# Two gate projections of a convolution branch in blocks of seven products, and a z gate applied four heads later

## The chip, the core and the metric

The kernel is one decoder layer for 256 tokens, and runs on one core of a Trainium2 chip. The metric is the device time of the core in microseconds; 1037.4 us is the median of three runs of the kernel before (1037.0 to 1037.94).

## The reference

All arithmetic is float32. A normalised input `h` (256 x 2048) is projected by one wide matrix, and the pieces feed two branches, attention over 16 heads and a short causal convolution with three taps. Each branch has a gate, and two further gates merge the branches:

```python
proj = jnp.einsum('bsd,de->bse', h, w_in)
# q_a, c_kv, k_rope, z_mla, c_in, b_gate, c_gate, z_conv, g_mla, g_conv = split(proj)
attn = _causal_mla_attention(q_nope, q_rope, k_nope, k_rope, v)      # 16 heads of 128
attn = attn.reshape(b, s, MLA_WIDTH) * jax.nn.silu(z_mla)
y_mla = jnp.einsum('bse,ed->bsd', attn, w_o_mla)
u = c_gate * c_in
conv = sum(conv_w[k] * u_pad[:, k:k + s] for k in range(CONV_K))
y_conv = jnp.einsum('bse,ed->bsd', b_gate * conv * jax.nn.silu(z_conv), w_o_conv)
merged = jax.nn.sigmoid(g_mla) * y_mla + jax.nn.sigmoid(g_conv) * y_conv
out = jnp.einsum('bsd,de->bse', merged, w_out)
x = x + _rmsnorm(out, post_norm_g)
```

The pieces that matter here are the seven projections of 2048 columns each: `z_mla`, `c_gate`, `c_in`, `z_conv`, `b_gate`, `g_mla`, `g_conv`.

## The kernel before, in words

**Three matmuls for a product.** TensorE works on pairs (hi, lo) of a rounded part and a rest. `product` (L253) issues three matmuls of 128 x 512 for one product: hi by hi, hi by lo, lo by hi. Each megabyte of weights (a unit) is loaded by SP into one of three `raw` buffers; ScalarE (ACT) copies it to `whi` (L269) and VectorE (DVE) subtracts to get `wlo` (L270). `whi` and `wlo` have three buffers each, and `take(i)` asks for the split of unit i+1 before unit i is used (`ahead`, L228). So the split of a unit can begin when the unit three places ahead of it has been used up, and must be done when its own turn comes.

**Plain projections.** A projection of 512 columns for all tokens is four units (quarters); each quarter is 2 token tiles x 4 k x 3 = 24 matmuls (`quarter`, L688). It fills two PSUM banks, one per token tile, which its evacuation must free before the next such projection can write them: the tag `cv` has two banks.

**The heads' stage** (L822 to 908) runs 16 heads. Each head's scores, softmax, transposition (by DVE in 32 x 32 pieces, then out to DRAM and back by DMAs of the POOL queue: `turned`, L345) and `values` leave TensorE nothing to do for long stretches, so plain projections are put between: before each four heads one projection of `z` (`gates`), and in each head the four quarters of one projection of the convolution branch (`channels`), in the order c_gate, c_in, z_conv, b_gate. A projection is evacuated in `channels_done` (L727): c_gate by a scaled copy on ACT; c_in and b_gate by a multiplication on DVE (L737); z_conv by a sigmoid on ACT (L734) and then L737 on DVE, so that both engines read its banks. `z` goes in the same way (L706, L707) into the very place of the attention output, is turned, and `values` multiplies each head's result into it (L682). The taps (`taps`) bring shifted rows and tap weights by POOL's DMAs and combine them on DVE (L770).

**Blocks of seven products.** The merge gates `g` (L956, `gate_block`, four blocks of 1024 columns) use a scheme that takes, for a pair of k (a "pair" unit), seven products in place of eight; a "whole" unit takes eight. A pair unit needs more splitting: `split_pair` (L204) makes three more weight sums `tf` on DVE (L212) and splits these too (`thi`, `tlo`). `gate_kinds` says which of a block's eight units are pairs: two in the first block, three in each of the others. All four blocks lie behind the heads, and their results `sg` stay in SBUF.

**Then** come the output projections of both branches (`sq`, 768 matmuls), the merge, and the last projection (`out`). A scheduler sets the order of instructions of an engine where `keep_in_program_order` does not; each engine then works strictly in that order.

## Time and profile before

| | |
|---|---|
| median of 3 runs | 1037.4 us |
| the profiled execution | 1037.89 us |
| its span | 1036.1 us |
| TensorE (PE) busy | 1022.2 us, 4661 matmul records |
| VectorE busy | 738.4 us |
| ScalarE busy | 530.6 us |
| POOL busy | 180.9 us |
| heads' stage | about 98 to 599 us |
| merge gates' blocks | 599.9 to 767 us |
| output projections `sq` | 767.2 to 941.3 us |

The profile shows one execution; the span is what the instructions cover, and the 1.8 us between it and the execution's time lie around them. In a group of instructions "busy" counts overlapping instructions once, and the mean is that of one instruction's own duration. A wait is put down to the instruction that released it.

### The profile page before, as it was taken

The numbers are of one execution on the slowest core, as the hardware profiler recorded it, in microseconds if no ns is written. First come the engines' busy times: TensorE is split into PE (matmuls) and PEld (weight loads), VectorE is DVE, ScalarE is ACT, GpSimd is POOL, SyncE is SP. The second block draws the span as 40 slices with busy tenths as digits, with TensorE's granted clock in tenths as the row PEclk, the third lists the DMA queues.
The fourth block names the chain that finished last, engine by engine and source line by source line (L and its number), as shares of the span: only waits on it lengthen the run. The fifth ranks groups of instructions, "written<-read, shape, count | busy, mean of one in ns | idle before, by whom it ended". The sixth has DMA issues, their size and how long they took to land.

```text
span 1036.1 us, 12480 instructions
## 1 busy us (share of the span) xinstructions
PE 1022.2 (99%) x4661; PEld 851.2 (82%) x4661; DVE 738.4 (71%) x960; ACT 530.6 (51%) x681; POOL 180.9 (17%) x345
## 2 busy tenths in 40 slices
PE   9999999999999999999999999999999999999997
PEld 8887888888888888888888888888888888888885
DVE  7578768776777767686678798898885455656562
ACT  7756546545556455464554645464664333443451
POOL 7620320204211241212222220000000000322000
PEclk9999999999999999999999999999999999999999
DMA  8755766668576676757576665555555555776842
GB/s 326 310 183 199 249 194 232 202 220 286 200 251 218 203 247 222 244 210 257 188 287 226 240 233 204 206 201 203 203 203 203 185 185 206 240 251 239 318 163 81
DMA packets 41948, 231.00 MB, mean 223 GB/s; under 512 B 7520, under 2 KB 8224, under 8 KB 18976
## 3 DMA queue, kind: packets, MB, share of 16 engines
q1 hardware_dynamic: 29808, 197.54, 53.5%
q0 software_dynamic: 11648, 29.38, 9.1%
q10 hardware_dynamic: 432, 3.29, 0.8%
q8 instruction: 36, 0.59, 0.2%
q14 instruction: 24, 0.20, 0.1%
HBM read 214.48 MB, written 11.53 MB: 218 GB/s over the span
## 4 chain that ended last, share of the span: by engine, by line
PE 95%; DVE 3%; issue 1%; ACT 1%; DVEq 0%; POOL 0%; POOLq 0%
PE cv L90 32%; PE sq L90 17%; PE g L90 16%; PE z L90 8%; PE out L90 8%; PE qa L90 2%; PE qn L90 2%; PE ckv L90 2%; PE kn L90 2%; PE vv L90 2%; DVE wlo L270 1%; PE sc L90 1%; PE o L90 1%; PE qr L90 1%; ACT whi L269 0%
## 5 line engine op out<-in xcount | busy, mean ns | idle before, releaser
L270 DVE TENSOR_TENSOR wlo<-raw,whi 128x1024 fp32r<-128x1024 f32 (+2 forms) x279 | 398.5, 1452 | 213.3 <-ACT whi L269 212.3
L269 ACT ACTIVATE whi<-raw 128x1024 fp32r<-128x1024 f32 (+2 forms) x281 | 336.4, 1233 | 344.2 <-issue 104.9
L90 PE MATMUL cv<-whi,x_both 128*128 128x512 f32 x1024 | 323.4, 390 | 2.9 <-DVE cv_w L737 2.9
L90 PEld LDWEIGHTS cv<-whi,x_both 128*128 128x128 f32 x1024 | 192.3, 188 | 43.1 <-DVE cv_w L737 4.0
L90 PE MATMUL cv<-wlo,x_both 128*128 128x512 f32 x512 | 199.7, 390 | 0.0
L90 PE MATMUL g<-whi,x_both 128*128 128x512 f32 x380 | 122.4, 389 | 0.0
L90 PEld LDWEIGHTS cv<-wlo,x_both 128*128 128x128 f32 x512 | 96.2, 188 | 18.7
L90 PEld LDWEIGHTS g<-whi,x_both 128*128 128x128 f32 x380 | 71.4, 188 | 14.7
L90 PE MATMUL z<-whi,x_both 128*128 128x512 f32 x256 | 80.6, 390 | 0.0
L90 PE MATMUL sq<-whi,x_both 128*128 128x512 f32 x256 | 79.0, 389 | 0.0
L90 PE MATMUL sq<-whi,cv_both 128*128 128x512 f32 x256 | 79.0, 389 | 0.0
L90 PE MATMUL out<-whi,x_both 128*128 128x512 f32 x256 | 79.0, 389 | 0.0
L356 POOL DMA_DIRECT2D far<-via x64 | 35.3, 558 | 223.8 <-DVE via L349 222.9
L90 PE MATMUL g<-wlo,x_both 128*128 128x512 f32 x190 | 73.9, 389 | 0.0
L356 POOL DMA_DIRECT2D far<-sg x32 | 17.5, 552 | 301.7 <-DVE sg L1045 259.7
L90 PEld LDWEIGHTS sq<-whi,x_both 128*128 128x128 f32 x256 | 48.1, 188 | 10.0
L90 PEld LDWEIGHTS sq<-whi,cv_both 128*128 128x128 f32 x256 | 48.1, 188 | 10.0
L90 PEld LDWEIGHTS out<-whi,x_both 128*128 128x128 f32 x256 | 48.1, 188 | 9.9
L90 PEld LDWEIGHTS z<-whi,x_both 128*128 128x128 f32 x256 | 48.1, 188 | 9.9
L90 PE MATMUL z<-wlo,x_both 128*128 128x512 f32 x128 | 49.8, 389 | 0.0
L90 PE MATMUL sq<-wlo,x_both 128*128 128x512 f32 x128 | 49.8, 389 | 0.0
L90 PE MATMUL sq<-wlo,cv_both 128*128 128x512 f32 x128 | 49.8, 389 | 0.0
(241 smaller groups left out, 1356.4 us busy)
## 6 DMA issues: line engine op xcount, KB each, us to landing
raw<-wcv_dram SPq DMA_DIRECT2D x64, 1024.0 KB, 5.3
raw<-wsq_dram SPq DMA_DIRECT2D x48, 1024.0 KB, 4.8
raw<-wg_dram SPq DMA_DIRECT2D x32, 1024.0 KB, 4.7
raw<-wz_dram SPq DMA_DIRECT2D x16, 1024.0 KB, 4.8
raw<-wqk_dram SPq DMA_DIRECT2D x8, 1024.0 KB, 5.9
cw<-cwr_dram POOLq DMA_DIRECT2D x24, 256.0 KB, 6.4
raw<-wc_dram SPq DMA_DIRECT2D x4, 1024.0 KB, 10.0
raw<-wv_dram SPq DMA_DIRECT2D x4, 1024.0 KB, 5.2
```

Of the source, the lines that this page charges most:

```text
L90: return tc.keep_in_program_order(nc.tensor.matmul(*a, **kw))
L269: a = nc.scalar.activation(hi, src, AF.Copy)
L270: b = nc.vector.tensor_tensor(lo, src, hi.bitcast(F32), op=ALU.subtract)
L356: tc.keep_in_program_order(nc.gpsimd.dma_start(out=f[i], in_=m))
```

## The change

`z_conv` and `b_gate` are no longer computed between the heads. Of the five plain projections with four parts each, three stay (`z`, `c_gate`, `c_in`): twelve projections of 512 columns (`FILLS`), four quarters ahead of the heads, two to three in each head. `z_conv` and `b_gate` become four blocks of 1024 columns in front of the four of the merge gates (`BLOCKS`), all by the scheme with seven products; `PLACES` gives each block's pair units (1, 3, 3, 2, 2, 3, 3, 3). In a pair unit DVE's two splits now stand one behind the other.

`z` is now evacuated by one activation (Silu, into `z_now`), turned in two steps, and multiplied into the attention output by `gates_weigh` four heads after its own four; the last one inside the first block. `values` no longer multiplies. The taps' steps are placed anew and take both token tiles with one load of the tap weights. The gate of the convolution branch, `w` = silu(z_conv) x b_gate, is a tile of 256 x 2048; the product of the convolution with it and its transposition move to the `sq` stage (`channels_steps`). The merge gates leave SBUF: each of 16 tiles is written to DRAM by POOL's queue (`gate_far`) and read back two at a time in the `sq` stage (`gate_tiles`).

The core of the diff:

```diff
+    order = ["fill"] * 4 + first
...
+        if u == "fill":
+            f, i = divmod(len(u_fill), 4)
+            j, n = FILLS[f]
+            u_fill.append(add(wz[j, i] if n == 2 else wcv[2 * j + n, i]))
         else:
-            u_head[i][j] = add(wcv[i, j])
...
         nc.scalar.activation(hi[:, :512], t[:, :512], AF.Copy)
-        split_act(thi[:, :, :], tlo[:, :, :], tf[:, :, :])
-        nc.vector.tensor_tensor(lo[:, :], t[:, :], hi[:, :].bitcast(F32), op=ALU.subtract)
+        nc.scalar.activation(thi[:, :, :], tf[:, :, :], AF.Copy)
+        tt(lo[:, :], t[:, :], hi[:, :].bitcast(F32), op=ALU.subtract)
+        tt(tlo[:, :, :], tf[:, :, :], thi[:, :, :].bitcast(F32), op=ALU.subtract)
...
-        f = temp("f")
-        whole(f[:, :], o)
-        nc.vector.tensor_tensor(at, f[:, :].rearrange("p (t i x) -> p t i x", t=NT, i=4), at, op=ALU.mult)
+        t = temp("half")
+        nc.scalar.activation(t[:, :], o[:, S:], AF.Copy)
+        a, b = (v.rearrange("p (t i x) -> p t i x", t=NT, i=4) for v in (o[:, :S], t[:, :]))
+        nc.vector.tensor_tensor(at, a, b, op=ALU.add)
...
-            cv_ps["now"] = [bank(f"cv{h}_{t}", tag="cv", bufs=2) for t in range(NT)]
-        quarter(cv_ps["now"], take(u_head[h][i]), i)
-        if i == 3:
-            channels_done(*divmod(h, 4))
-
-    def channels_done(j, n):
-        for t in range(NT):
-            ps, r = cv_ps["now"][t], r_col[:, t : t + 1]
-            w, u = cv_w[:, t, :], cv_t[:, j, t, :]
+            cv_ps["now"] = [bank(f"cv{f}_{t}", tag="cv", bufs=2) for t in range(NT)]
+        quarter(cv_ps["now"], take(u_fill[f]), i, between)
...
             if n == 0:
                 nc.scalar.activation(u, ps[:, :], AF.Copy, scale=r)
-            elif n == 2:
-                nc.scalar.activation(w, ps[:, :], AF.Sigmoid, scale=r)
-            if n:
-                dst = u if n == 1 else w
-                nc.vector.scalar_tensor_tensor(dst, ps[:, :], r, dst, op0=ALU.mult, op1=ALU.mult)
-
...
-    def channels_join(j, t):
-        u, w = cv_t[:, j, t, :], cv_w[:, t, :]
-        nc.vector.tensor_tensor(u, u, w, op=ALU.mult)
-
-        via = temp("cw", (P, 512), bufs=2) if t else temp("mv2", (P, 512), bufs=1, tag="mv2x")
-        go, come = turned(u, via, 4)
-        go()
-        return lambda: come(u)
...
+            elif n == 1:
+                nc.vector.scalar_tensor_tensor(u, ps[:, :], r, u, op0=ALU.mult, op1=ALU.mult)
+            else:
+                nc.scalar.activation(z_now[:, t, :], ps[:, :], AF.Silu, scale=r)
+        if n == 1:
+            steps = taps(j)
+            tap_steps.extend([steps] * 3 if j == 3 else [steps, None, steps, None, steps])
+        elif n == 2:
+            z_steps.append(gates_turn())
...
+    def gates_turn():
+        steps = [turned(z_now[:, t, :], temp("via", (P, 512), bufs=2), 4) for t in range(NT)]
+        for go, _ in steps:
+            go()
+        yield
+        for t, (_, come) in enumerate(steps):
+            come(z_now[:, t, :])
+        yield
+
+    def gates_weigh(v):
+        for t in range(NT):
+            at = at_t[:, v, t, :]
+            tc.keep_in_program_order(nc.vector.tensor_tensor(at, at, z_now[:, t, :], op=ALU.mult))
...
+            fill()
         if h < H - 1:
             score(h)
         if h:
-            channels(h, 0)
...
+            fill()
...
+        step()
         for i in made[h]:
             make(*i)
+        if h > 1 == at:
+            make("v", v)
+            pt = turn(ps_by_head.pop(h - 1))
...
+        if h < H - 1:
+            arrive()
...
+        fill()
...
+        if h and not h > 1 == at:
+            pt = turn(ps_by_head.pop(h - (h < H - 1)))
+        if v and at == HV - 1:
+            gates_weigh(v - 1)
...
+        step()
+        if h and not h > 1 == at:
+            fill()
+        if h:
+            values(h - (h < H - 1), pt)
...
+        for job in jobs.get(len(kinds), ()):
+            job()
         for m, t, half, other in ((2, 0, 0, p1[:, :]), (3, 0, 1, u[:, 0]), (4, 1, 0, u[:, 2]), (0, 1, 1, u[:, 1])):
-            o = 1024 * b + 512 * half
-            g = sg[:, n, t, o : o + 512]
-            tt(g, ps[m][:, :], other, op=ALU.add)
-            nc.scalar.activation(g, g, AF.Sigmoid, scale=r_col[:, t : t + 1])
...
+            done(ps[m][:, :], other, t, half)
...
+    def open_spool():
+        bstack.close()
+        sp = main.enter_context(tc.tile_pool(name="sp", bufs=1, side="right"))
+        spool["pool"] = sp
+        spool["w"] = sp.tile([P, NT, D], F32, name="cv_w")
...
+    def zc_done(b):
+        def done(ps, other, t, half):
+            o = D // 2 * b + 512 * half
+            silu(spool["w"][:, t, o : o + 512], ps, other, t)
+
+        return done
+
+    def b_done(b):
+        def done(ps, other, t, half):
+            o = D // 2 * b + 512 * half
+            w = spool["w"][:, t, o : o + 512]
+            nc.vector.tensor_tensor(other, ps, other, op=ALU.add)
+            nc.vector.scalar_tensor_tensor(w, other, r_col[:, t : t + 1], w, op0=ALU.mult, op1=ALU.mult)
+
+        return done
...
+    def g_done(n, b):
+        def done(ps, other, t, half):
+            c = 2 * b + half
+            g = spool["pool"].tile([P, 512], F32, name=f"sg{n}{c}{t}", tag="sg", bufs=4)
+            nc.vector.tensor_tensor(g[:, :], ps, other, op=ALU.add)
+            nc.scalar.activation(g[:, :], g[:, :], AF.Sigmoid, scale=r_col[:, t : t + 1])
+            gate_far[n, c, t] = dram.tile([P, 512], F32, name=f"gate{n}{c}{t}", tag=f"gate{n}{c}{t}", bufs=1)
+            tc.keep_in_program_order(nc.gpsimd.dma_start(out=gate_far[n, c, t][:, :], in_=g[:, :]))
+
+        return done
...
+    jobs = {1: [gates_step], 2: [gates_step], 5: [lambda: gates_weigh(NV - 1)], 7: [open_spool]}
+    for n, (name, b) in enumerate(BLOCKS):
+        put = g_done(*divmod(b, 2)) if name == "g" else {"zc": zc_done, "b": b_done}[name](b)
+        if n == len(BLOCKS) - 1:
+            jobs = {6: [lambda: split_branch(0), lambda: split_branch(1)], 7: [lambda: split_branch(2)]}
+        block(n, put, jobs)
+        jobs = {}
...
+    def channels_steps(i):
+
+        if i < 8:
+            j, t = divmod(i, NT)
+            u = cv_t[:, j, t, :]
+            w = spool["w"][:, t, 512 * j : 512 * j + 512]
+            tc.keep_in_program_order(nc.vector.tensor_tensor(u, u, w, op=ALU.mult))
+            go, channels_come[i] = turned(u, spool["pool"].tile([P, 512], F32, name="via_c", tag="via", bufs=2)[:, :], 4)
+            go()
+        if 2 <= i < 10:
+            j, t = divmod(i - 2, NT)
+            channels_come.pop(i - 2)(cv_t[:, j, t, :])
+        if 5 <= i < 13:
+            split_channels(i - 5)
...
+            if n == 0:
+                channels_steps(4 * c + kk)
...
+    def gate_tiles(n, c):
+        gs = []
+        for t in range(NT):
+            g = spool["pool"].tile([P, 512], F32, name=f"gs{n}{c}{t}", tag="sg", bufs=4)
+            tc.keep_in_program_order(nc.gpsimd.dma_start(out=g[:, :], in_=gate_far[n, c, t][:, :]))
+            gs.append(g[:, :])
+        return gs
...
+FILLS = [(0, 0), (0, 1), (1, 0), (1, 1), (0, 2), (2, 0), (2, 1), (1, 2), (3, 0), (2, 2), (3, 1), (3, 2)]
+BLOCKS = [("zc", 0), ("zc", 1), ("b", 0), ("b", 1), ("g", 0), ("g", 1), ("g", 2), ("g", 3)]
+PLACES = [(4,), (0, 2, 4), (0, 2, 4), (0, 3), (0, 3)] + [(0, 2, 4)] * 3```

Where a projection's banks are freed. Before, on DVE, at the end of a z_conv projection, that of head 6 counted from 0 (L737 reads the two banks `cv_0` and `cv_1`; `mv` and `cw` are taps, `f` and `half` are evacuations of q, k and v parts, `pt` are the turned weights of a head):

```order
L270 TENSOR_TENSOR wlo_2781<-raw_2745,whi_2780 128x1024 x2
L770 TENSOR_TENSOR cv_f<-cv_f,cw 128x512
L270 TENSOR_TENSOR wlo_2853<-raw_2778,whi_2852 128x1024 x2
L770 TENSOR_TENSOR cv_f<-cv_f,mv_2583 128x512
L423 TENSOR_TENSOR f<-qr_2753,half 128x256
L270 TENSOR_TENSOR pt<-p,pt 128x384
L737 SCALAR_TENSOR_TENSOR cv_w<-cv_0_2627,r_both,cv_w 128x512
L737 SCALAR_TENSOR_TENSOR cv_w<-cv_1_2628,r_both,cv_w 128x512
```

Now the two-engine evacuation is gone from the heads; this is ACT at the end of a z projection, the nearest thing to it:

```order
L268 ACTIVATE pt<-p 128x384
L268 ACTIVATE whi_2190<-raw_2096 128x512
L716 ACT_TABLE_LOAD
L716 ACTIVATE z_now<-cv_0_1827,r_both 128x512
L716 ACTIVATE z_now<-cv_1_1828,r_both 128x512
L268 ACTIVATE whi_2228<-raw_2188 128x1024 x2
L680 ACTIVATE half<-o_2144 128x256
```

The two banks are read by two activations of one engine, with a table load in front.

Ahead of the scores of the first head, on DVE, up to the split of `qr`, which the scores need. Before:

```order
L270 TENSOR_TENSOR wlo_951<-raw_908,whi_950 128x1024
L270 TENSOR_TENSOR kn<-f,kn 128x256
L270 TENSOR_TENSOR vv_lo<-vv_0_916,vv_hi 128x512
L270 TENSOR_TENSOR kn<-f,kn 128x256
L423 TENSOR_TENSOR f<-qr_881,half 128x256
L270 TENSOR_TENSOR vv_lo<-vv_1_931,vv_hi 128x512
L486 TENSOR_TENSOR rp_a<-f,cos_t 128x256
L489 TENSOR_TENSOR rp_b<-f,sin_t 32x256 x4
L270 TENSOR_TENSOR wlo_1025<-raw_948,whi_1024 128x1024 x2
L490 TENSOR_TENSOR f<-rp_a,rp_b 128x256
L270 TENSOR_TENSOR wlo_1065<-raw_1022,whi_1064 128x512
L270 TENSOR_TENSOR qr<-f,qr 64x256 x2
```

And now, on the same engine and at the same place:

```order
L269 TENSOR_TENSOR wlo_949<-raw_906,whi_948 128x512
L422 TENSOR_TENSOR f<-kn_0_840,half 128x256
L422 TENSOR_TENSOR f<-kn_1_841,half 128x256
L269 TENSOR_TENSOR vv_lo<-vv_0_914,vv_hi 128x512
L269 TENSOR_TENSOR kn<-f,kn 128x256 x2
L422 TENSOR_TENSOR f<-qr_879,half 128x256
L485 TENSOR_TENSOR rp_a<-f,cos_t 128x256
L488 TENSOR_TENSOR rp_b<-f,sin_t 32x256 x4
L269 TENSOR_TENSOR vv_lo<-vv_1_929,vv_hi 128x512
L489 TENSOR_TENSOR f<-rp_a,rp_b 128x256
L269 TENSOR_TENSOR wlo_1015<-raw_946,whi_1014 128x1024 x2
L269 TENSOR_TENSOR qr<-f,qr 64x256 x2
```

Behind the split of the unit ahead of these rows (`wlo_911` before, `wlo_909` now) stood two quarters of 2 x 1024 (`wlo_951`, whose first half stands two rows above the excerpt, and `wlo_1025`) and one half-unit of 512; now one quarter (`wlo_1015`) and one half-unit of 512. One quarter's split no longer stands in front of `qr`.

In the blocks, on DVE, at the border of two blocks. Before (first to second block; L1000 frees the first block's banks, `tf` and `raw` are a pair unit's sums):

```order
L212 TENSOR_TENSOR tf_5700<-raw_5669 128x1024
L1000 TENSOR_TENSOR sg<-g_4_5381,u 128x512
L1000 TENSOR_TENSOR sg<-g_0_5384,u 128x512
L212 TENSOR_TENSOR raw_5669<-raw_5669,tf_5700 128x512
L212 TENSOR_TENSOR tf_5700<-raw_5669 128x512
L220 TENSOR_TENSOR wlo_5699<-raw_5669,whi_5698 128x2048
L270 TENSOR_TENSOR wlo_5738<-raw_5696,whi_5737 128x2048
L270 TENSOR_TENSOR tlo_5702<-tf_5700,thi_5701 128x1536
```

And now, from the first `b_gate` block to the second, where each of four evacuations has a second operation (L983):

```order
L210 TENSOR_TENSOR wlo_4981<-raw_4948,whi_4980 128x2048
L210 TENSOR_TENSOR tlo_4984<-tf_4982,thi_4983 128x1536
L982 TENSOR_TENSOR p_4911<-g_2_4749,p_4911 128x512
L269 TENSOR_TENSOR wlo_5036<-raw_4978,whi_5035 128x2048
L983 SCALAR_TENSOR_TENSOR cv_w<-p_4911,r_both,cv_w 128x512
L982 TENSOR_TENSOR u<-g_3_4750,u 128x512
L982 TENSOR_TENSOR u<-g_4_4748,u 128x512
L982 TENSOR_TENSOR u<-g_0_4751,u 128x512
L983 SCALAR_TENSOR_TENSOR cv_w<-u,r_both,cv_w 128x512 x3
L269 TENSOR_TENSOR wlo_5063<-raw_5033,whi_5062 128x2048
```

The `tlo` of a pair unit, which stood behind the next unit's `wlo`, now stands directly behind its own; three second operations stand behind the last bank's read and in front of the next split.

264 lines of the change are left out of this document (105 added, 159 removed).

## The prediction

> **What bounds the kernel now.** First the page's table of busy times and its row of the granted clock:
>
> ```profile
> PE 1022.2 (99%) x4661; PEld 851.2 (82%) x4661; DVE 738.4 (71%) x960; ACT 530.6 (51%) x681; POOL 180.9 (17%) x345
> PEclk9999999999999999999999999999999999999999
> ```
>
> TensorE is busy for 1022.2 of 1036.1 us, so what is left outside it is 13.9 us, and no other engine comes near. Whether that busy time is work is told by its waits:
>
> ```profile
> PE cv L90 <- DVE cv_w L737: 2.9, 4, 0.9
> PE sc L90 <- DVE qr L270: 1.7, 1, 1.7
> PE idle L90 <- POOL hpi L293: 1.1, 1, 1.1
> PE g L90 <- DVE tlo L270: 0.4, 1, 0.4
> ```
>
> These are all (total, times, longest): 6.1 us; the other 7.8 us are the end, behind the last matmul (941.30 + 87.05 = 1028.35 in the next view). Four waits of up to 0.9 us stand at the release of a projection's banks, one at the first head's scores, one in the blocks. The chain of work that ended last gives the price of one matmul, and the table of stages (span, PE, PEld, DVE, ACT, POOL busy, clock, DMA share, GB/s) what cover there is in each:
>
> ```profile
> 767.22 174.08 PE sq L90 x768
> 941.30 87.05 PE out L90 x384
> 233.00:369.00 136.00, 135.16 (x635) 113.09 (x635) 100.71 (x162) 72.25 (x110) 29.33 (x54) 1.00 0.68 229
> 599.90:766.70 166.80, 166.41 (x735) 137.48 (x734) 145.55 (x123) 91.82 (x78) 5.48 (x10) 1.00 0.59 208
> 767.20:941.30 174.10, 174.10 (x770) 144.21 (x769) 100.40 (x77) 70.98 (x51) 16.43 (x30) 1.00 0.60 212
> ```
>
> 174.08 / 768 = 0.2267 us from matmul to matmul. The second row is one round of four heads; the third the merge gates' blocks, where VectorE is already busy for 145.55 / 166.8 = 87% and TensorE waited 0.4 us.
>
> **TensorE's own work.** Before: 16 + 4 plain projections of 96 matmuls (1920), and four blocks of 192 less 3 for each of 11 pairs (735), 2655 together. Now 12 projections (1152) and eight blocks with 20 pairs (1536 - 60 = 1476), 2628. All are 128 x 512. 27 fewer at 0.2267 us: **-6.1 us**, on the path, since TensorE has next to no idle time to absorb it. The Trainium skill (TensorE: Matmul & The Clock Gate, "Back-to-back issue gap") gives a sustained spacing of about 131 ns for matmuls of 512 columns; the trace disagrees with its 227 ns, and it decides. By the page's figure the term would be an estimated -3.5 us.
>
> **Waits that go.** The release of a z_conv projection's banks, in the chain and on the two engines that free them:
>
> ```profile
> 301.88 3.40 PE cv L90 x15
> 305.28 0.95 PE sc L90 x8
> 306.26 0.75 DVE cv_w L737
> 307.06 0.96 PE cv L90 x3
> 303.12 1.28 ACT L734 ACT_TABLE_LOAD   x1
> 304.42 0.69 ACT L734 ACTIVATE cv_w<-cv,r_both 128x512 f32<-128x512 f32 x1
> 305.80 0.55 DVE L270 TENSOR_TENSOR pt<-p,pt 128x384 fp32r<-128x384 f32 x1
> ```
>
> The first bank is complete 12 matmuls (2.7 us) ahead of 305.28, at 302.6. A table load and the sigmoid end at 305.1, then VectorE is at other work until 306.26, and its multiplication lets TensorE in at 307.06. Two engines in a row are longer than the 2.7 + 0.95 us of cover. z_conv leaves the heads, so these four waits go: **-2.9 us** (bounds -2.9 and 0, if others come in their place; those I count below). z is now freed by ACT alone: 1.28 + 0.69 = 2.0 us, under 2.7.
>
> For the first scores, VectorE's queue:
>
> ```profile
> 83.24 2.36 DVE L270 TENSOR_TENSOR wlo<-raw,whi 128x1024 fp32r<-128x1024 f32 x2 [0.57 <-ACT whi L269]
> 93.50 2.36 DVE L270 TENSOR_TENSOR wlo<-raw,whi 128x1024 fp32r<-128x1024 f32 x2
> 96.83 0.87 DVE L270 TENSOR_TENSOR qr<-f,qr 64x256 fp32r<-64x256 f32 x2
> ```
>
> From 83.24 to `qr` it is busy without a break, and one quarter's split (2.36 us) no longer stands there. That is more than the 1.7 us waited: **-1.7 us** (bounds -1.7 and 0).
>
> **The heads' stage, the risk.** The cover shrinks. A round of four heads held 20 quarters and now holds 11 on average (3 + 2 + 3 + 3). TensorE loses 9 x 24 x 0.2267 = 49.0 of 136 us: 87.0. VectorE's durations:
>
> ```profile
> L737 DVE SCALAR_TENSOR_TENSOR cv_w<-cv,r_both,cv_w 128x512 f32<-128x512 f32 x16 | 11.7, 745 | 1.0 <-PE cv L90 1.0
> L1000 DVE TENSOR_TENSOR sg<-g,u 128x512 f32<-128x512 f32 x12 | 7.7, 683 | 0.0
> L682 DVE TENSOR_TENSOR at_f<-f,at_f 128x256 f32<-128x256 f32 x16 | 6.8, 422 | 0.3
> ```
>
> From its 100.7 us go 9 splits at 2.36 (21.2), four evacuations of z_conv and b_gate and two of z at 0.745 (4.5), the products with `w` and their transpositions (four operations of 512, 2.7 at 0.683) and one of two operations of each head's result (4 x 0.42 = 1.7); two multiplications by z come (1.4). That leaves 72.0 of 87.0 us, 83%, where it was 74%. What is spare is 15.0 us for 16 units (11 quarters, two of q and k, two of rotary q, one of v), 0.94 us a unit. The blocks' stage of before lived with 21.25 us for 32 units, 0.66 each, and waited 0.4 us. So throughput suffices; what remains is single late releases. There are 12 projections whose banks are handed on, all freed by one engine. The trace had 12 such projections in `cv` too (c_gate, c_in, b_gate), and none of them made TensorE wait. Bounds: 0, and 12 x 0.9 = 10.8 us. I take **+2.0**, two waits of the known size, since VectorE has less spare time and some projections now follow each other without scores between; nearer to the lower end because that row has the same mechanism.
>
> **The blocks.** A pair unit costs VectorE, from these rows, 2.29 + 1.75 + 1.22 + 0.69 + 0.69 = 6.64 us, a whole one 2.29:
>
> ```profile
> L220 DVE TENSOR_TENSOR wlo<-raw,whi 128x2048 fp32r<-128x2048 f32 x11 | 25.2, 2291 | 2.7 <-ACT whi L218 2.7
> L270 DVE TENSOR_TENSOR tlo<-tf,thi 128x1536 fp32r<-128x1536 f32 x11 | 19.3, 1754 | 1.2 <-ACT thi L269 1.0
> L212 DVE TENSOR_TENSOR tf<-raw 128x1024 f32<-128x1024 f32 x11 | 13.4, 1219 | 0.0
> L212 DVE TENSOR_TENSOR tf<-raw 128x512 f32<-128x512 f32 x11 | 7.6, 690 | 0.3
> L212 DVE TENSOR_TENSOR raw<-raw,tf 128x512 f32<-128x512 f32 x11 | 7.5, 685 | 0.2
> ```
>
> Eight blocks: twice 145.55, less two pairs (2 x 4.35), plus eight second operations of b_gate (6.0): 288.4 us against TensorE's 1476 x 0.2267 = 334.6: 86%, as before. Twice the length at the same load gives twice 0.4 us: **+0.4**. Bounds: -0.4, because the `tlo` that was waited for no longer stands behind the next `wlo`; and +2.2, if b_gate's three second operations (3 x 0.745) hold up one split.
>
> **Edits at nothing.** The last z is turned in the first block; its multiplication stands four units (some 21 us) behind.
>
> ```profile
> L356 POOL DMA_DIRECT2D far<-sg x32 | 17.5, 552 | 301.7 <-DVE sg L1045 259.7 <-DVE sg L349 41.2 <-issue 0.8
> far<-sg POOLq DMA_DIRECT2D x32, 64.0 KB, 3.0
> sg<-far POOLq DMA_DIRECT2D x8, 256.0 KB, 3.8
> ```
>
> Eight issues (4.4), landing (3.0), two issues (1.1) and landing (3.8) make 12.3 us; behind a late one VectorE's next splits would queue. The other z have several projections' time. The 16 gate tiles out and back are 0.25 MB each: 4 MB in blocks of four over 167 us is 25 GB/s on top of 208, where the stage of the heads has 229. In the `sq` stage a product, a transposition and a split are added to some units; VectorE has 100.4 of 174.1 us there, and 16 x 0.7 = 11 more fit. POOL issues five or six DMAs a unit at 0.55, some 3 us of 5.4. If that cover failed, `cv_both` would be late at the first use, three units after its last split.
>
> **The sum.** The profiled execution's own time is 1037.89, 0.5 above the median of 1037.4. 1037.9 - 6.1 - 2.9 - 1.7 + 2.0 + 0.4 = 1029.6; against the median **1029.1 us**. With no wait left but the start it would be 1037.4 - 6.1 - 2.9 - 1.7 - 0.4 = 1026.3.
>
> **Rivals.** 0.2% of this kernel, 2.1 us, is about what a measurement can tell from no change; so faster means under 1035.3 and slower over 1039.5.
>
> - *VectorE bound in the heads by ScalarE's copies (slower).* Each split on VectorE waits for the copy `whi`, and that copy waits for a free buffer, that is for TensorE. If VectorE stands still for a time at each of 16 units, the spare 0.94 us a unit is used up and the heads become a chain of copy and split. Beyond 0.94 every 0.1 us costs 1.6 us a round, 6 us over 3.75 rounds; about 1.1 us a unit eats the gain. At 1.25 us it is (20.0 - 15.0) x 3.75 = 19 us, about 1048. For: this row, 1.95 us on average, and half a unit's copy alone is 1.05:
>
> ```profile
> DVE wlo L270 <- ACT whi L269: 212.3, 109, 4.7
> L269 ACT ACTIVATE whi<-raw 128x1024 fp32r<-128x1024 f32 x192 | 192.2, 1051 | 160.8 <-issue 87.2 <-PE cv L90 48.3 <-PE z L90 19.1
> ```
>
>   Against: those waits stood where VectorE had nothing else to do, and the blocks did with less to spare. Chance 0.10.
> - *Every hand-over waits (no change).* The upper bound of 10.8 instead of 2.0: 1037.9. Chance 0.12: 0.05 of it under 1035.3, with fewer or shorter waits, 0.06 about no change, 0.01 slower.
> - *The waits only move.* The releases of z and c_in, with a table load or behind taps, are late as those of z_conv were, and the first scores wait as before: 1037.4 - 6.1 + 0.4 = 1031.7, 0.15. For: the same tap operations stand on VectorE around the heads' ends. Against: the 2.0 us of ACT alone.
> - That TensorE's count does not fall is excluded by the instructions themselves.
>
> **How the numbers follow.** The forecast has 0.63, its own range 1026.3 to 1033. Faster: 0.63 + 0.15 + 0.05 = 0.83; same 0.06; slower 0.01 + 0.10 = 0.11. The low end is the floor of 1026.3; the high end 1037.0 takes in the better half of the second rival and leaves out the first.
>
> **What would show it.** Right: TensorE 6 us less busy or the same chain with 27 matmuls fewer; no `cv_w` and no `qr` among its waits; VectorE near 83% in the rounds and 86% in the blocks; at most a few waits under 1 us. Wrong: a row of TensorE waiting for `wlo` many times in the heads (first rival), for a bank at each projection (second), or over 2 us at block borders; a wait for DMAs on `z_now` or `gs` would break the edits at nothing.

## The result, and the profile after

The changed kernel takes 1029.58 us (median of four runs, 1027.61 to 1030.09) against 1037.38 of the kernel before: a ratio of 0.9921, interval 0.9904 to 0.9938. The profiled execution is the run of 1027.61 us, 2 us below the median of its kernel; its span is 1025.6 us. That distance turned out to be part of the answer (below). First the page's table of busy times and TensorE's waits (total, times, longest):

```profile
PE 1014.0 (99%) x4634; PEld 844.6 (82%) x4634; DVE 777.9 (76%) x972; ACT 536.5 (52%) x667; POOL 191.5 (19%) x365
```

```profile
PE vv L90 <- DVE f L422: 2.2, 2, 1.9
PE idle L90 <- POOL hpi L292: 1.1, 1, 1.1
PE qa L90 <- ACT whi L268: 0.4, 1, 0.4
```

TensorE has 4634 matmul records where it had 4661: 27 fewer. The waits for `cv_w`, for `qr` and for `tlo` are all gone. Two places are new. `vv`, the projection of v, waits for VectorE's `f`, 1.9 us in head 5 and 0.3 us in head 13. The 0.4 us of `qa` at the very start come and go from profile to profile (they are missing in experiments 2, 6, 9 and 12), and nothing below rests on them.

The chain that ended last (start, length, what) shows the blocks as a single piece, and around 200 us the new wait:

```profile
197.89 2.70 PE kn L90 x16
...
202.19 0.34 DVE f L422
202.57 5.75 PE vv L90 x24
...
422.13 334.60 PE g L90 x1476
756.73 174.08 PE sq L90 x768
```

All eight blocks run without any gap, 1476 matmuls at 0.2267 us. In head 5 TensorE has finished `kn` and stands until VectorE has written `f`, which empties the bank that `vv` needs. The stages, in the same columns as before:

```profile
103.30:189.65 86.35, 86.35 (x425) 73.17 (x425) 71.54 (x136) 48.09 (x88) 23.42 (x43) 1.00 0.67 224
422.10:589.40 167.30, 167.30 (x740) 138.49 (x739) 144.34 (x121) 86.52 (x68) 7.51 (x14) 1.00 0.60 213
589.40:756.70 167.30, 167.30 (x740) 138.53 (x739) 141.18 (x117) 91.53 (x76) 7.03 (x13) 1.00 0.63 222
756.70:930.80 174.10, 174.10 (x770) 144.16 (x769) 109.75 (x93) 72.01 (x51) 48.56 (x89) 1.00 0.75 265
```

A round of four heads takes 86.35 us with VectorE at 71.54 (83%); the blocks have VectorE at (144.34 + 141.18) / 334.6 = 85%; the `sq` stage carries its added work with TensorE busy throughout.

Why VectorE writes `f` late in head 5 is told by POOL's DMA issues, and by VectorE (start, length, instruction, in brackets the idle time before it and what ended it):

```profile
181.40 2.12 POOL L755 DMA_DIRECT2D mv<-cv_f  x4
183.51 1.10 POOL L755 DMA_DIRECT2D cw<-cwr_dram  x2
186.29 0.54 POOL L755 DMA_DIRECT2D cw<-cwr_dram  x1 [1.68 <-DMA far<-via]
```

```profile
196.98 0.69 DVE L758 TENSOR_TENSOR mv<-mv,cw 128x512 f32<-128x512 f32 x1 [1.47 <-DMA cw<-cwr_dram]
...
202.11 0.74 DVE L422 TENSOR_TENSOR f<-qn,half 128x256 f32<-128x256 f32 x2
```

POOL issues four shifted rows and three rows of tap weights; the last is issued at 186.29 and is used at 196.98, 10.7 us later. VectorE, which works in order, stands 1.47 us for it, and `f` stands several instructions behind. So the theory is that a tap load which lands late sets TensorE's new wait through VectorE's order. Its rival: VectorE simply has too much to do in the heads, and waits appear wherever it is late.

### The profile page after: what moved, and what is told of

It is laid out like the page before. It is cut to its first block, busy times and chain, and to the rows that moved or that the text cites. A ratio compares the mean times of both kernels' runs of the same rounds, so it can differ in the third digit from the quotient of the medians.

```text
span 1025.6 us, 12524 instructions
## 1 busy us (share of the span) xinstructions
PE 1014.0 (99%) x4634; PEld 844.6 (82%) x4634; DVE 777.9 (76%) x972; ACT 536.5 (52%) x667; POOL 191.5 (19%) x365
## 3 DMA queue, kind: packets, MB, share of 16 engines
q0 software_dynamic: 13248, 34.63, 10.7%
## 4 chain that ended last, share of the span: by engine, by line
PE 98%; DMA 1%; DVE 1%; ACT 0%; SPq 0%; issue 0%; DVEq 0%
PE g L90 33%; PE cv L90 26%; PE sq L90 17%; PE out L90 8%; PE vv L90 2%; PE kn L90 2%; PE qn L90 2%; PE ckv L90 2%; PE qa L90 2%; PE sc L90 1%; PE qr L90 1%; PE o L90 1%; DMA raw<-xw_dram 1%; PE kr L90 0%; DVE og L1132 0%; SPq L159 0%
## 5 line engine op out<-in xcount | busy, mean ns | idle before, releaser
L269 DVE TENSOR_TENSOR wlo<-raw,whi 128x1024 fp32r<-128x1024 f32 (+2 forms) x238 | 375.3, 1595 | 162.5 <-ACT whi L268 161.8
L268 ACT ACTIVATE whi<-raw 128x1024 fp32r<-128x1024 f32 (+2 forms) x240 | 316.6, 1346 | 296.9 <-PE sq L90 95.2
L90 PE MATMUL g<-whi,x_both 128*128 128x512 f32 x784 | 251.2, 389 | 0.0
L90 PE MATMUL cv<-whi,x_both 128*128 128x512 f32 x768 | 242.9, 390 | 0.0
L90 PEld LDWEIGHTS g<-whi,x_both 128*128 128x128 f32 x784 | 147.1, 188 | 30.4
L90 PEld LDWEIGHTS cv<-whi,x_both 128*128 128x128 f32 x768 | 144.2, 188 | 29.4
L90 PE MATMUL g<-wlo,x_both 128*128 128x512 f32 x392 | 152.5, 389 | 0.0
L90 PE MATMUL cv<-wlo,x_both 128*128 128x512 f32 x384 | 149.7, 390 | 0.0
L90 PEld LDWEIGHTS g<-wlo,x_both 128*128 128x128 f32 x392 | 73.6, 188 | 15.4
L90 PEld LDWEIGHTS cv<-wlo,x_both 128*128 128x128 f32 x384 | 72.2, 188 | 13.9
L90 PE MATMUL sq<-whi,x_both 128*128 128x512 f32 x256 | 79.0, 389 | 0.0
L90 PE MATMUL sq<-whi,cv_both 128*128 128x512 f32 x256 | 79.0, 389 | 0.0
L90 PE MATMUL out<-whi,x_both 128*128 128x512 f32 x256 | 79.0, 389 | 0.0
L212 ACT ACTIVATE whi<-raw 128x1536 fp32r<-128x1536 f32 x20 | 29.8, 1491 | 61.7 <-PE g L90 44.4
L90 PEld LDWEIGHTS sq<-whi,x_both 128*128 128x128 f32 x256 | 48.0, 188 | 10.1
L90 PEld LDWEIGHTS sq<-whi,cv_both 128*128 128x128 f32 x256 | 48.0, 188 | 10.1
L90 PEld LDWEIGHTS out<-whi,x_both 128*128 128x128 f32 x256 | 48.0, 188 | 10.0
L210 DVE TENSOR_TENSOR wlo<-raw,whi 128x2048 fp32r<-128x2048 f32 x20 | 45.8, 2292 | 7.5 <-ACT whi L216 7.5
L90 PE MATMUL sq<-wlo,x_both 128*128 128x512 f32 x128 | 49.8, 389 | 0.0
L90 PE MATMUL sq<-wlo,cv_both 128*128 128x512 f32 x128 | 49.8, 389 | 0.0
```

The source lines that it names most:

```text
L90: return tc.keep_in_program_order(nc.tensor.matmul(*a, **kw))
L210: tc.keep_in_program_order(nc.vector.tensor_tensor(*a, op=op))
L212: nc.scalar.activation(hi[:, 512:], t[:, 512:], AF.Copy)
L268: a = nc.scalar.activation(hi, src, AF.Copy)
L269: b = nc.vector.tensor_tensor(lo, src, hi.bitcast(F32), op=ALU.subtract)
```

## The experiments

Every time stands beside runs of the kernel before on the same chip, whose medians lay at 1037.31 to 1037.59.

**1. The kernel before, with the banks of z_conv freed by ScalarE alone.** Silu in place of the sigmoid, so that VectorE's multiplication falls away:

```diff
-                nc.scalar.activation(w, ps[:, :], AF.Sigmoid, scale=r)
-            if n:
+                nc.scalar.activation(w, ps[:, :], AF.Silu, scale=r)
+            if n % 2:
```

> The kernel before, with one part of the change: the z_conv projection in the heads is evacuated by one activation (Silu) on ScalarE instead of a sigmoid on ScalarE and a multiplication on VectorE. Theory (the forecast's step: the release through two engines caused four waits): TensorE's waits for cv_w fall from 2.9 us to at most 0.3 and nothing takes their place, time down by 2.9 to 4.0 us from 1037.4, so about 1034. Rival (the waits only move): waits at the next projection's start appear instead, time within 1 us of 1037.4.

Measured 1033.64, ratio 0.9963 (0.995 to 0.9976): -3.7 us. Its waits:

```profile
PE sc L90 <- DVE qr L270: 1.7, 1, 1.7
...
PE g L90 <- DVE tlo L270: 0.4, 1, 0.4
```

The four waits for `cv_w` are gone and the rest is as it was. The cause was the two engines in a row; the price was 0.8 us more than the 2.9 us in the table of waits. The chains of the two kernels show why: behind such a wait 48 matmuls took 11.18 us (the kernel before), and at the same place without it 0.27 us less (this run).

```profile
307.06 11.18 PE cv L90 x48
```

```profile
305.07 10.91 PE cv L90 x48
```

**2. One pair unit in each block.** The changed kernel with 8 pairs instead of 20, so 36 matmuls more:

```diff
-PLACES = [(4,), (0, 2, 4), (0, 2, 4), (0, 3), (0, 3)] + [(0, 2, 4)] * 3
+PLACES = [(4,)] * 8
```

> The changed kernel with one pair unit in each of the eight blocks instead of 1, 3, 3, 2, 2, 3, 3, 3: 8 pairs instead of 20, 36 matmuls more, 12 times 4.35 us less work on VectorE. Theory (TensorE alone sets the blocks' time, 0.2267 us for a matmul, VectorE at 85% hidden): blocks 334.6 + 8.2 = 342.8 us, time up by 8.2 us. By a price of 131 ns it would be up by 4.7 us. Rival (pair units also cost TensorE something through VectorE): up by clearly less than 8 us.

Measured 1035.2, ratio 0.998 (0.9971 to 0.999). The blocks in its chain:

```profile
422.57 342.76 PE g L90 x1512
```

342.76 - 334.60 = 8.16 us for 36 matmuls: 0.2267 us each. Matmuls that are left out are worth exactly their pitch. The medians are only 5.6 us apart, since three of the four runs of the changed kernel have something in them that its profile lacks (experiment 11).

**3. v's projection ahead of the first filling quarter** in heads 5, 9 and 13:

```diff
-        order += ["fill"] + made[h] + [("v", h // HV)] * (h > 1 == at) + ["fill"] * (1 + (h > 0 and not h > 1 == at))
+        order += [("v", h // HV)] * (h > 1 == at) + ["fill"] + made[h] + ["fill"] * (1 + (h > 0 and not h > 1 == at))
...
+        if h > 1 == at:
+            make("v", v)
...
-            make("v", v)
```

> The changed kernel with the value projections vv of heads 5, 9 and 13 moved ahead of the head's first filling quarter, so that they no longer follow the q and k projections directly; the order of weight units follows. Theory (the only new waits, 2.2 us at vv in heads 5 and 13, are a bank of q or k that VectorE frees late, at the one place where no filling matmuls stand between): both waits go, profiled span 1025.6 - 2.5 = about 1023. Rival (VectorE is short in those heads whatever the order): the waits reappear at another place there, span within 0.5 us of 1025.6.

Measured 1031.12, ratio 0.9942 (0.9925 to 0.9959): 1.5 us above the changed kernel, with intervals that overlap, and not faster. `vv` no longer waits, but another does, in head 13:

```profile
PE o L90 <- DVE pt L269: 4.4, 1, 4.4
```

The expectation failed. The wait of `vv` can be taken away by the order of TensorE's work, but the projection was also the cover of the step after it. This run does not tell the late load from a VectorE with too much to do.

**4. The tap weights loaded ahead of the shifted rows.** The three DMAs for `cw` are issued in front of the four for `mv`:

```diff
+            if t:
+                for d, cw in enumerate(cws):
+                    bring(cw, cwr[2 - d : 3 - d, 512 * j : 512 * (j + 1)].to_broadcast([P, 512]))
             for d in (1, 2):
...
-            if t:
-                for d, cw in enumerate(cws):
-                    bring(cw, cwr[2 - d : 3 - d, 512 * j : 512 * (j + 1)].to_broadcast([P, 512]))
```

> The changed kernel with the loads of the tap weights issued ahead of the shifted rows on the POOL queue, some 2 us earlier. Theory (the wait of 1.9 us at vv in head 5 comes from VectorE standing 1.5 us at a tap whose weights land late): that wait falls to at most 0.5 us, the other (0.3 us, head 13) stays, span 1025.6 - 1.5 = about 1024. Rival (VectorE's load in that head, not the load's landing): TensorE's wait in head 5 stays above 1.2 us.

Measured 1031.7, ratio 0.9946 (0.9931 to 0.9961): 2.1 us above the changed kernel, again with intervals that overlap; the profiles differ by 3.9 us of span (1029.5 against 1025.6). The waits of TensorE, a piece of the chain (the DMA from issue to landing), and VectorE's row:

```profile
PE vv L90 <- DVE f L422: 4.6, 2, 4.3
```

```profile
185.65 13.55 DMA mv<-cv_f
...
204.88 7.33 PE vv L90 x24
```

```profile
199.27 0.69 DVE L758 TENSOR_TENSOR cv_f<-cv_f,cw 128x512 f32<-128x512 f32 x1 [3.68 <-DMA mv<-cv_f]
```

Now a shifted row is the last of the seven to be issued; it lands after 13.55 us, VectorE stands 3.68 us instead of 1.47, and TensorE 4.3 instead of 1.9. The repair failed, but the dose speaks for the late load: what is last in POOL's queue decides, and TensorE's wait grows with VectorE's stand at it. And `vv`'s 24 matmuls took 7.33 us instead of 5.75; experiment 11 shows the same and the clock behind it.

**5. The changed kernel once more**, unchanged.

> The changed kernel once more, unchanged, for a second profile. Theory A (the tap's landing decides): the wait of vv in head 5 is as long as the last of seven loads of POOL's queue makes it, and that varies from run to run; its usual runs lie 2 us above the profiled one (1029.6 against 1027.6) because this wait is longer in them. A profile of 1029 to 1030 then shows a wait of vv of 3 to 4.5 us, with the granted clock below 1.00 in the 10 us behind it; one of 1027.6 shows about 1.9 us again. Theory B (the 2 us have nothing to do with the wait): a profile of 1029 to 1030 shows the wait at 1.9 us and the lower clock in another place. Median 1029 to 1030 either way.

Measured 1028.37 (1026.73 to 1029.42), ratio 0.9909 (0.9895 to 0.9924). The profiled run is one of 1027.47 us:

```profile
PE vv L90 <- DVE f L422: 1.8, 2, 1.5
```

```profile
196.85 0.69 DVE L758 TENSOR_TENSOR mv<-mv,cw 128x512 f32<-128x512 f32 x1 [1.08 <-DMA cw<-cwr_dram]
```

The same load was issued at 186.38 and used at 196.85: 10.5 us, 0.2 less than in the first profile, and TensorE's wait 0.4 us shorter. The landing does vary from run to run. This profile does not show a run of 1029 to 1030.

**6. The taps' products half a head later.** In the changed kernel the products come one step further behind their loads, so that in heads 5 and 9 they stand behind the evacuation of q and k:

```diff
-            tap_steps.extend([steps] * 3 if j == 3 else [steps, None, steps, None, steps])
+            tap_steps.extend([steps] * 3 if j == 3 else [steps, None, None, steps, None, steps])
```

> The changed kernel, with the tap products of the first three column groups one half head later behind their loads, so that in heads 5 and 9 they stand behind the evacuations of the q and k projections. Theory A (VectorE stands in order behind a late tap load): the wait of vv in head 5 goes (1.9 us, and 0.28 us of restart), nothing of over 1 us takes its place, the profiled span is 1023.0 to 1024.0, and the median falls by 3.5 to 4.5 us to 1025 to 1026.5, since the longer waits of the usual runs go too; the wait in head 13 (0.3 us) stays. Theory B (VectorE has too much to do there, whatever it waits for): the same work is only moved, a wait of 1.5 to 4 us appears at another bank in heads 5 to 7, and the median stays at 1028 to 1031.

Measured 1025.57 (1025.24 to 1025.92), ratio 0.9884 (0.9869 to 0.9899); the interval has no part in common with that of the unchanged repeat on the same chip, 0.9895 to 0.9924. The only wait beside the start's is the one of 0.3 us in head 13. The chain in head 5:

```profile
197.83 2.79 PE kn L90 x16
200.62 5.47 PE vv L90 x24
```

`vv` follows `kn` without a gap, at its ordinary 5.47 us, and no wait took the place of the old one. VectorE has just as much to do (777.7 us busy against 777.9). Theory A is confirmed, B would have moved the wait. The median lies where A put it, but the fall is 2.8 us against the repeat on this chip, less than the 3.5 to 4.5 that were expected from the first measurement. The four runs lie within 0.7 us, where those of the changed kernel spread over 2.5.

**7 and 8. More work for VectorE.** One, and then three, maxima of 512 elements behind each quarter from the fifth on; their results are used nowhere. This tests the first rival, the one that forecast slower:

```diff
+        if f >= 4:
+            for k in range(1):
+                tc.keep_in_program_order(
+                    nc.vector.reduce_max(warm[:, :], x_both[:, k, :].bitcast(F32), axis=mybir.AxisListType.X)
+                )
```

> The changed kernel with one more maximum of 512 elements on VectorE (0.6 to 0.7 us, its result is used nowhere) behind every quarter of a projection of the filling from the fifth on: 11 in a round of four heads, 7 us, where 86.35 - 71.54 = 14.8 us are free. Prediction's count (VectorE is slack by throughput, only single releases come late): 0 to +5 us on the median of the changed kernel, 1029 to 1035, TensorE's waits in the heads stay under 6 us in all. Rival 1 (the heads are nearly a chain of copy and split, so that any time of VectorE counts): at least half of the 28 us that are added come out, 1043 or more.

> The same with three such maxima behind each quarter: 33 in a round of four heads, 21 to 23 us, against 14.8 us free. Prediction's count: VectorE bounds the heads, 6 to 8 us over in each of four rounds, 1052 to 1064 in all, VectorE's share of the heads over 95%, and TensorE waits for it in many places. Rival 1: the chain was nearly full before, so all of the 88 us that are added come out, above 1085. If the free time were larger than counted: below 1045.

With one: 1029.33, ratio 0.9931 (0.9914 to 0.9948), 1.0 us above the unchanged repeat on that chip. The added group, and the first round of heads:

```profile
L710 DVE TENSOR_REDUCE warm<-x_both 128x1 f32<-128x512 f32 x44 | 29.8, 677 | 0.0
```

```profile
103.30:189.65 86.35, 86.35 (x424) 72.92 (x423) 78.95 (x152) 48.04 (x87) 23.36 (x43) 1.00 0.69 225
```

29.8 us of work on VectorE cost at most about 1.0 us (the intervals overlap): with 78.95 / 86.35 = 91% it still lets TensorE through. In head 5 `vv` does not wait at all, with more work for VectorE than before: there the last tap load landed 9.4 us after its issue, and VectorE did not stand for it. The wait in head 13 is 1.5 us long instead of 0.3. With three: 1069.78, ratio 1.0307 (1.0291 to 1.0322), 41.4 us more for 89.4 us of work. A stretch of the heads in that run (TensorE's costliest wait, for `pt`, is 23.7 us in five times, up to 8.5):

```profile
103.30:363.00 259.70, 242.56 (x1153) 203.24 (x1153) 245.22 (x453) 136.79 (x245) 58.49 (x108) 0.97 0.62 204
```

VectorE is at 94%, just under the 95% expected, and the granted clock, 0.97 there, is below 1 as well. The count of free time holds (one maximum fits, three do not), and the rival does not: its bill would have been half of 29.8 us and all of 89.4. The measured time lies 6 us above the upper end of what was expected for three; the mean clock of the whole run is 0.985 against 0.998, an estimated 14 us of 1066 by that ratio, and it was not counted.

**9. Three pairs in every block, with the late taps.** 24 pairs instead of 20, 12 matmuls fewer:

```diff
-PLACES = [(4,), (0, 2, 4), (0, 2, 4), (0, 3), (0, 3)] + [(0, 2, 4)] * 3
+PLACES = [(2, 4, 6)] + [(0, 2, 4)] * 7
```

> The changed kernel with the taps' products half a head later (as in the kernel before with that edit, 1025.6) and three pairs in every block: 24 pairs instead of 20, so 12 matmuls of 0.2267 us fewer. Theory A (TensorE bounds the blocks, VectorE's release of banks is slack): -2.7 us, 1022.5 to 1023.2, and the blocks' stage is 1464 x 0.22669 = 331.9 us in one piece. Theory B (four more pairs, 4 x 4.35 = 17 us more of VectorE, 91% of the blocks, use its slack up): waits of g in the first or the middle blocks, 1024 to 1028.

Measured 1042.77, ratio 1.0058 (1.0045 to 1.007): slower than the kernel before, 17 us above experiment 6. Its waits, a stretch in the first block, and VectorE in front of a wait of the fourth block:

```profile
PE g L90 <- DVE tlo L210: 15.6, 5, 5.4
```

```profile
422.00:465.00 43.00, 35.39 (x139) 28.11 (x139) 34.82 (x33) 18.14 (x16) 7.50 (x14) 0.87 0.59 205
```

```profile
568.72 2.08 DVE L983 SCALAR_TENSOR_TENSOR cv_w<-u,r_both,cv_w 128x512 f32<-128x512 f32 x3
...
571.31 2.29 DVE L210 TENSOR_TENSOR wlo<-raw,whi 128x2048 fp32r<-128x2048 f32 x1
573.51 2.29 DVE L269 TENSOR_TENSOR wlo<-raw,whi 128x2048 fp32r<-128x2048 f32 x1
575.71 1.76 DVE L210 TENSOR_TENSOR tlo<-tf,thi 128x1536 fp32r<-128x1536 f32 x1
```

Theory B of that expectation holds, and goes further than its numbers; the profiled run, of 1047.13 us, lies another 4.4 us above the median. The five waits are 4.9 and 2.5 us in the first block, 5.4 at the start of the second, and 1.4 each in the two blocks that follow one of b_gate. In all five cases VectorE makes the `tlo` behind the split of the next unit (`wlo` of L269), as in the rows above. In the changed kernel each of the 20 `tlo` stands directly behind its own `wlo`, and none is waited for; in the kernel before one of the 11 does not, and that is the one with the wait of 0.4 us.

In the first block VectorE has the end of the heads to do as well (the last taps, and z, for whose load it stands 1.8 us); behind a block of b_gate the pair at unit 2 gets its `tlo` after b_gate's second operations (L983) and two whole splits, at 577.47. VectorE's 34.82 / 43 = 81% in the first block is not spare room: the waits themselves lengthen that stretch, whose 139 matmuls would take 31.5 us at 0.2267 us. Behind the three long waits the granted clock falls to 0.50, behind the two short ones it does not:

```profile
461.80:464.80 3.00, 3.00 (x7) 2.42 (x8) 0.00 (x0) 0.00 (x0) 0.00 (x0) 0.50 0.87 360
577.50:580.50 3.00, 2.98 (x13) 2.48 (x14) 2.93 (x4) 0.63 (x1) 0.00 (x0) 1.00 0.87 363
```

Experiment 6 has the same late taps and its blocks are in one piece of 334.60 us, so the places of the pairs make the difference: the single pair of the first block, and the places 0 and 3 behind the b_gate blocks, keep `g` in one piece.

**10. The old order of two subtractions on the pairs' side** (`tlo` ahead of `lo`), in the changed kernel:

```diff
-        nc.scalar.activation(thi[:, :, :], tf[:, :, :], AF.Copy)
-        tt(lo[:, :], t[:, :], hi[:, :].bitcast(F32), op=ALU.subtract)
-        tt(tlo[:, :, :], tf[:, :, :], thi[:, :, :].bitcast(F32), op=ALU.subtract)
+        split_act(thi[:, :, :], tlo[:, :, :], tf[:, :, :])
+        nc.vector.tensor_tensor(lo[:, :], t[:, :], hi[:, :].bitcast(F32), op=ALU.subtract)
```

> The changed kernel with the order of two subtractions of the pairs' side as it was before (tlo ahead of lo). Theory A (the blocks now wait nowhere by other slack as well): 0, 1028 to 1030, no wait of g. Theory B (that order is what took the wait of 0.4 us for tlo away): +0.4 to +0.8, a wait of g for tlo of 0.4 to 0.8 us in the profile; hardly to be told from none by the time, so the profile decides.

Measured 1027.58, ratio 0.9902 (0.9889 to 0.9914). Its longest wait is 2.2 us, of `vv` in head 5. Behind it, and in the blocks:

```profile
202.95 5.74 PE vv L90 x24
...
422.49 334.60 PE g L90 x1476
```

No wait of `g`. But this run does not try what it was made for, because on VectorE the order is not the old one: each of the 20 `tlo` (L268) still stands directly behind its own `wlo` (L218) and ahead of the next unit's. At the place where the kernel before waited (the third unit of the second block of the merge gates):

```profile
636.62 2.29 DVE L218 TENSOR_TENSOR wlo<-raw,whi 128x2048 fp32r<-128x2048 f32 x1 [0.83 <-ACT whi L216]
638.83 1.75 DVE L268 TENSOR_TENSOR tlo<-tf,thi 128x1536 fp32r<-128x1536 f32 x1
```

The kernel before, with these very lines, has ten of its eleven `tlo` so. The lines of `split_pair` do not set the order; experiment 12 shows what does. The rest of the profile serves in the next experiment.

**11. Each gate tile written twice.** 16 DMAs of 256 KB more, the copies read by nobody:

```diff
+            twin = dram.tile([P, 512], F32, name=f"twin{n}{c}{t}", tag=f"twin{n}{c}{t}", bufs=1)
+            tc.keep_in_program_order(nc.gpsimd.dma_start(out=twin[:, :], in_=g[:, :]))
```

> The changed kernel with each of the 16 tiles of the merge gates written to memory twice, the second copy read by nobody: 4 MB more over 167 us (25 GB/s) and 16 more DMAs in POOL's queue. Theory A (the tiles' traffic is hidden): 0, 1028 to 1030, g in one piece of 334.6 us. Theory B (it is near to a limit): a wait of g for weights in the last four blocks, +1 us or more.

Measured 1029.25, ratio 0.9917 (0.9903 to 0.9931): no change that can be told. The blocks, and head 5 of this profile, a run of 1030.16 us:

```profile
PE vv L90 <- DVE f L422: 2.7, 2, 2.4
```

```profile
203.21 7.33 PE vv L90 x24
...
424.38 334.60 PE g L90 x1476
```

```profile
203.00:206.00 3.00, 2.79 (x7) 2.21 (x8) 3.00 (x5) 1.27 (x4) 3.00 (x7) 0.60 0.75 205
206.00:209.00 3.00, 3.00 (x12) 2.42 (x11) 1.61 (x5) 1.15 (x3) 0.24 (x1) 0.83 1.04 379
```

The tiles' traffic is hidden. By chance this profile caught what the first one lacked: the wait is 2.4 us, and behind it the granted clock is 0.60 and 0.83, so that `vv`'s 24 matmuls take 7.33 us, 1.6 us more than behind waits of 1.5, 1.9 and 2.2 us. In steps of 1 us the clock is 0.50 from 204 to 207 us and 0.99 right after. The instructions up to there are those of the changed kernel.

Six profiles now show the same tap load in head 5. VectorE stood for it 1.08 (experiment 5), 1.47 (the first profile), 1.72 (experiment 10), 1.75 (2), 1.92 (11) and, reordered, 3.68 us (4); TensorE waited 1.5, 1.9, 2.2, 2.2, 2.4 and 4.3 us. Every run has a mean granted clock of its own as well. Of the twelve runs of the changed kernel, its repeat and this experiment, the seven with a mean of 0.996 took 1029.27 to 1030.16 us, and the five with 0.998 took 1026.73 to 1028.35. A difference of 0.002 in 1027 us is 2 us, about what the halved clock cost here.

**12. Late taps, and a third pair at unit 5 behind the blocks of b_gate.**

```diff
-PLACES = [(4,), (0, 2, 4), (0, 2, 4), (0, 3), (0, 3)] + [(0, 2, 4)] * 3
+PLACES = [(4,), (0, 2, 4), (0, 2, 4), (0, 3, 5), (0, 3, 5)] + [(0, 2, 4)] * 3
```

> The changed kernel with the taps' products half a head later, and a third pair in the two blocks that follow a block of b_gate, at units 0, 3 and 5 (in place of 0 and 3; the run with 0, 2 and 4 there waited for tlo of unit 2, which VectorE began only behind the eight operations of b_gate's evacuation). The first block keeps its one pair. 22 pairs, 6 matmuls fewer than with the late taps alone: 1.36 us. Theory A (the place of a pair decides, not VectorE's share, 88% there): no wait of g, g in 1470 x 0.22669 = 333.2 us in one piece, 1024.0 to 1024.6. Theory B (VectorE's slack in these blocks is used up wherever the third pair stands): one or two waits of g of 2 to 5 us, 1026 to 1034.

Measured 1025.44 (1025.16 to 1025.64), ratio 0.9886 (0.9869 to 0.9902): the same as experiment 6 within the spread. The wait in the blocks, and the first and last piece of `g`:

```profile
PE g L90 <- DVE tlo L210: 0.8, 2, 0.4
```

```profile
419.77 177.53 PE g L90 x783
...
640.08 114.31 PE g L90 x503
```

From 419.77 to 754.39 are 334.6 us, as with six matmuls more. Two waits of 0.4 us and the restarts behind them took back the 1.36 us. The first lies at unit 3 of the second of the two changed blocks, the other at unit 2 of the block behind it, whose own places, 0, 2 and 4, were not changed. In both, `tlo` stands behind the next unit's split again; for the second:

```profile
633.55 2.29 DVE L210 TENSOR_TENSOR wlo<-raw,whi 128x2048 fp32r<-128x2048 f32 x1
636.06 2.29 DVE L269 TENSOR_TENSOR wlo<-raw,whi 128x2048 fp32r<-128x2048 f32 x1 [0.21 <-ACT whi L268]
638.27 1.75 DVE L210 TENSOR_TENSOR tlo<-tf,thi 128x1536 fp32r<-128x1536 f32 x1
```

This is the wait of the kernel before come back: that too had a block whose last pair was unit 5 (`gate_kinds` there has 3 and 5) in front of one with 0, 2 and 4, and waited 0.4 us at unit 2. Experiment 6 differs from this run in the two places alone and has no such wait. So the place of a pair decides both the order on VectorE and the wait, 0.4 us here against 1.4 with the pair at unit 2 behind b_gate (experiment 9); A is half right. At unit 5 a third pair is not free; other places were not tried.

## Why the prediction was right

The forecast was 1029.1, measured 1029.58. Its steps:

- **TensorE's 27 matmuls, -6.1 us: right.** 4634 records against 4661; the blocks in one piece at 0.2267 us; and experiment 2 gives 8.16 us for 36.
- **The four waits for `cv_w`, -2.9 us: right in cause, too small.** Experiment 1 has -3.7 us for them alone; the sum left out the restart behind each wait, 0.27 us.
- **The first scores, -1.7 us: as forecast, but not tried by itself.** The wait is gone from the profile of after and from all profiles of its variants, except for 0.4 us in the run with three maxima (experiment 8).
- **New waits in the heads, +2.0 us: right size in the profile, wrong place, and wrong in the median.** The prediction looked at the hand-over of the `cv` banks, and counted from two waits of the known size there. None of the twelve projections waited at all. The one real wait is at an `mm` bank in front of `vv` in head 5, behind a tap load that lands late (1.9 us, and 0.3 in head 13). What the prediction missed is that a wait on VectorE's side can be a DMA's: it costed VectorE's work per unit, and did not follow POOL's queue to the heads in which `vv` comes directly behind q and k. Experiment 6 takes the wait away: 1025.57 against 1028.37 on the same chip, so it costs 2.8 us in that median, and 4.0 by the median of the first measurement, which was taken apart from it.
- **The blocks, +0.4 us: wrong sign, small.** The old 0.4 us went instead of doubling; -0.4 was the lower bound. What failed is the scaling with the length of the stage: the wait did not come from VectorE's share, but from one `tlo` behind the next unit's split, as the lower bound had it. Apart from experiment 8, whose VectorE is overloaded, all nine waits for `tlo` in the traces (one each in the kernel before and in experiment 1, five in 9, two in 12) have this order, and no other `tlo` has it. But the swap of two lines in `split_pair` is not what removed it: experiment 10 is without the swap and has no such wait, experiment 12 has the swap and has the wait. The places of the pairs did it. The upper bound's mechanism (b_gate's second operations hold up a split) is real: experiment 9 shows it behind the b_gate blocks.
- **Edits at nothing: right** where they were tried. The gate tiles could even be written twice (experiment 11); `sq` is in one piece of 174.08 us as before. The last z is turned beside the first block without harm as long as that block has a single pair; with three, VectorE stands 1.8 us for it there (experiment 9).
- **From the profiled run to the median, -0.5 us: wrong.** The profiled run of before lay 0.5 us above its median, that of after 2.0 below. In its own profile the change brought 1037.89 - 1027.61 = 10.3 us where the sum said 8.3; the median then had 2 us that this profile doesn't show. They are time at a lowered clock: the runs of 1029 to 1030 us have a mean of 0.996, that of the profile 0.998. Experiment 11 shows such a run, with the clock halved behind a wait of 2.4 us in head 5, and with the wait taken away (experiment 6) all four runs have 0.998 or more and lie within 0.7 us. That the clock fell in head 5 in the other runs too is likely, but no profile of one of the unchanged kernel was taken.

So it is luck that the total came out within 0.5 us: the waits that went were put 1.6 us too low (0.8 each for `cv_w` and in the blocks), and the new wait brought a slowed clock with it, 2 us in the median, that no term of the sum had.

The rivals. VectorE bound in the heads: refuted, by 83% in the round and by experiment 7, where 91% still lets TensorE through; its threshold is real, as experiment 8 shows, but lies beyond. Every hand-over waits: not one does. The waits only move: refuted for z, c_in and the scores, though one wait of a new kind did appear.

## What to carry to other kernels

A share of busy time tells whether an engine's work fits, not where it comes late. VectorE's work at 91% of TensorE's time cost at most 1 us in the heads (experiment 7); in the blocks of experiment 9, 302.4 us against the 331.9 that the matmuls need, again 91%, it cost some 17 us, because it came bunched. Such a share is read against the time that the work would take without waits, since the waits lengthen the stretch. And an edit of program lines is no experiment on an engine's order until the trace shows another order. When a step is moved, follow each load that it waits for to the queue that issues it, and ask what stands behind the waiting instruction on its engine; half a head more between a tap's load and its use was worth 2.8 us here, nearly half of what 27 matmuls fewer brought. A wait that one profile shows as 2 us can cost 4 in another run, 2.4 us and 1.6 more of slowed matmuls behind it (experiment 11), so compare the profiled run with the spread of the others before explaining a median.

## What was not expected of the hardware

**The clock answers to short pauses.** Behind waits of TensorE of 1.5, 1.9 and 2.2 us the next 24 matmuls took 5.73 to 5.75 us; behind 2.4 and 4.3 us they took 7.33, with granted clocks of 0.60 and 0.83 in the two stretches of 3 us behind the wait of 2.4 us. In experiment 9 the clock is 0.50 for 3 us behind waits of 2.5, 4.9 and 5.4 us, and 1.00 behind those of 1.4 us. The 5.74 us are a matter of restarting and not of the clock: undisturbed, 24 matmuls took 5.47 us, and behind the wait of only 0.3 us in head 13 they took 5.74 as well, at a granted clock of 1.00. The Trainium skill (TensorE: Matmul & The Clock Gate, "Part 1: The HAM clock gate") has the clock halved after an idle window of about 3.4 us that runs freely. The trace agrees that a pause brings it down, and that the same program may or may not meet it, but here 2.4 us were enough, less than that window.

**A load's landing.** Of seven loads of up to 256 KB that POOL issues in a row the last took longest to land: 9.4 to 11.3 us for the tap weights in six profiles with this order of issue (10.7 in the first, where the four shifted rows ahead of them took 4.7 to 8.4), 13.55 us for a shifted row when that was last. What makes it so long was not tried.
